# Neighbourhood attention block: squares, bias tables, last product order and residual loads rearranged

## The chip, the cores and the metric

The kernel runs on one core of a Trainium2 chip. The metric is the device time of one execution in microseconds; the time of a kernel is the median of its runs. Inputs and outputs are float32.

## What is computed

One layer of an encoder on 512 tokens (8 rows of 64 columns) of width 2048, with 16 heads of width 128. Cut to what matters:

```python
h = rms_norm(x, norm_pre)
q, k, v, z = split(h @ w_in, 4)            # 2048 -> 4 x 2048
s = q . k * 128**-0.5 + rpb[dr, dc]        # a window of 8 rows x 16 columns per token
o = softmax(s) @ v
y = (o * silu(z)) @ w_out                  # 2048 -> 2048
x = x + rms_norm(y, norm_post)
```

## The kernel before

The two large matrix products make up nearly all the work. Each float32 operand is split into a high part `hi` (a cast on ScalarE, line 241 for weights) and a rest `lo` (a subtraction on VectorE, line 242), and a product is three matmuls of 512 columns per output block: hi·hi, lo of the activations times hi, hi times lo of the weights.

The work is a list of 512 weight tiles of 128x512 (256 KB each), called products here and numbered m. It is cut into ten steps. Step 0 and step 8 are plain (`PLAIN`): 32 products of twelve matmuls each, 16 for each half of the output columns; step 0 computes the first pair of heads, step 8 half of the output product. Steps 1 to 7 (a pair of heads each) and step 9, the last one (`LAST`, products 456 to 511), save an eighth of the matmuls by a seven-product scheme: seven passes of eight products with six matmuls, called A11, S1, A12, N2, A22, N4 and N3 after their left operand (numbers 0 to 6, P1 to P7 in the change's title). They add into three pairs of accumulators X, Y and Z (`chain`, line 258); `combine` (331) reads these at the end of a pass. In the last step the table `LATE` (51) gives the passes another order, A11, S1, N2, A22, N4, N3, A12; its last pass, A12, runs block by block (line 299), and both its operands lie in the tiles `a{k}_2` and `a{k}_3`, whose former contents were used up by then.

Weights come in two ways. A pass that takes a tile of the input as it is (`is_raw`, 205) loads it into one of four buffers `raw` (`load_raw`, 216), about six products ahead, each buffer after the tile four loads earlier has been used. Sums of tiles are kept in eight resident tiles `T[k]`, shown as `t`: passes S1, N2 and A22 add a raw tile to T (line 234) and take the sum; A22 then reloads T (247); N4 uses a raw tile and adds it to T behind its own split (249), and N3 takes that sum. `prep` (227) does all this two products ahead of the matmuls; `hi` and `lo` have three buffers, so a cast waits until the product three before has run.

All loads of weights, activations and residuals are issued by SP in order; an SP instruction that waits holds up those behind it. GpSimd's queue issues the bias rows and the gated outputs. A scheduler orders the instructions of each engine from the program order and its own estimate, so rows stand somewhat off the program's order; engines run their rows in order. Calls through `sync`, `dve` and `act` (`InOrder`, 56) keep their program order.

Beside the products, `at(m, f)` hangs the other work on product m:

- RMSNorm statistics: `square_x` (174) loads x in eight blocks `sq` of 512 KB, and ScalarE squares and sums them. `rstd` (185) makes the factor `rc` from the sums: two small VectorE operations and a power on GpSimd. `take_first` (283) copies step 0's accumulators to SBUF times `rc`: the first half (n = 0) at product 28 and after, the second at 31.
- Bias: `load_bias` (441) loads overlapping rows of a head's table by GpSimd's queue (184 KB); `bias` (447) reverses them, adds a mask and writes the table `bm`, three VectorE operations per head; `add_bias` (472) reads it.
- The end: `finish` (653) squares a block of y, multiplies it by the post-norm gain, and collects the sums; `final` (669) scales it, adds the residual `xres` (16 tiles of 256 KB, names are row block and column block) and stores it. `load_res` (677) issues the residual loads: those of row blocks 2 and 3 with each product of pass S1, of 1 with every second product of N2, of 0 in N3.

Of the kernel before, what the change touches and what calls it, by code (L numbers as in the profile page):

```python
# [15 lines left out]
P = 128  # L16
# [33 lines left out]
B11, B12, B21, B22 = range(4)  # L50
LATE = (0, 1, 3, 4, 5, 6, 2)
NRAW = 4
# [14 lines left out]
@with_exitstack  # L67
def na_block(ctx: ExitStack, tc: tile.TileContext, xT, x, gpre, gpost, w, rpb, mask, out):
    nc = tc.nc
# [29 lines left out]
    nc.gpsimd.memset(mhalf, -0.5)  # L99
    mask_sb = cp.tile([P, 3, 32], F32, name="mask_sb")  # L100
    edge = {}
# [22 lines left out]
    def load_t(step, q, k):  # L124
        nc.sync.dma_start(T[k], w[step, q, k])

# [83 lines left out]
    seq = [m for m in range(N) if is_raw(m)]  # L210
    for i, m in enumerate(seq):
        e = max(m - 6 if m < N - KH else 0, seq[i - NRAW] if i >= NRAW else 0)
        if m > 2:
            at_prep.setdefault(e, []).append(m)

    def load_raw(m):
        raws[m] = wp.tile([P, L], F32, tag="raw", name=f"raw{m}", bufs=NRAW)
        step, p, k = where(m)
        if step in PLAIN:
            src = w[step, (B11, B12, B21, B22)[p + 2 * (k // KH)], k % KH]  # L220
        else:
            src = w[step, (None, B12, B21, B22, B21, B22)[p], k]
        nc.sync.dma_start(raws[m], src)
# [3 lines left out]
    def prep(m):  # L227
        step, p, k = where(m)
        plain = step in PLAIN
        if step == 0 and p == 0:  # L230
            take_x(k)
        src = raws.pop(m) if is_raw(m) else T[k]
        if not plain and p in (1, 3, 4):
            nc.vector.tensor_tensor(T[k], T[k], src, ALU.add)  # L234
# [6 lines left out]
        nc.scalar.copy(hi, src)  # L241
        nc.vector.tensor_tensor(lo, src, hi.bitcast(F32), ALU.subtract)  # L242
# [40 lines left out]
    def take_first(n, j):  # L283
        c = C.setdefault(0, {})
        name = ("11", "12", "21", "22")[n + j // 2 * 2]
        if j % 2 == 0:
            c[name] = pair(f"c{name}_0")
        nc.scalar.activation(c[name][:, j % 2, :], U[n][j], AF.Copy, scale=rc[:, j : j + 1])

# [41 lines left out]
    def combine(step, p):  # L331
# [14 lines left out]
        elif p == 3:  # L346
            c["22"] = pair(f"e_{step}")
            for s in range(2):
                nc.vector.tensor_tensor(c["22"][:, s, :], u[s], c["12"][:, s, :], ALU.subtract)
            nc.vector.tensor_tensor(c["21"], c["22"], c["21"], ALU.subtract)  # L350
        elif p == 4:
            for s in range(2):
                nc.vector.tensor_tensor(c["22"][:, s, :], u[s], c["22"][:, s, :], ALU.add)
        elif p == 5:
            for s in range(2):
                nc.vector.tensor_tensor(c["12"][:, s, :], u[s], c["12"][:, s, :], ALU.subtract)  # L356
            for s in range(2):
                if step == LAST:
                    finish(3, s, c["12"][:, s, :])
                else:  # L360
                    scale_c(c["12"], s, 0)
        elif step == LAST:
            c["11"] = pair(f"c11_{step}")
            for s in range(2):
                dve.tensor_tensor(c["21"][:, s, :], u[s], c["21"][:, s, :], ALU.subtract)
                dve.tensor_tensor(c["22"][:, s, :], c["22"][:, s, :], u[s], ALU.subtract)
                finish(2, 2 + s, c["21"][:, s, :])
                finish(3, 2 + s, c["22"][:, s, :])
# [72 lines left out]
    def load_bias(h):  # L441
        raw = sp.tile([P, L], F32, tag="braw", name=f"braw{h}")
        src = bass.AP(rpb.tensor, rpb.offset + h * 15 * TBL, [[1, 16], [TBL, 8], [1, 7 * TBL + 32]])
        nc.gpsimd.dma_start(raw[:, 0 : 7 * TBL + 32], src)  # L444
        bm_of[h] = (raw, sp.tile([P, 3, 256], F32, tag="bm", name=f"bm{h}"))

    def bias(h, i):
        raw, bm = bm_of[h]
        rev = bass.AP(raw.tensor, raw.offset + 7 * TBL + 31, [raw.ap[0], [-1, 32], [-TBL, 8]])
        nc.vector.tensor_tensor(  # L450
            bm[:, i, :].rearrange("p (a b) -> p a b", b=8),
            rev,
            mask_sb[:, i, :].unsqueeze(2).to_broadcast([P, 32, 8]),
            ALU.add,
        )

# [15 lines left out]
    def add_bias(h, a):  # L472
# [3 lines left out]
        for i in ((0, 1), (3, 2))[a]:  # L476
# [5 lines left out]
                in0=s_of[h, a][:, base + lo : base + hi],  # L482
                in1=bm_of[h][1][:, (0, 1, 1, 2)[i], lo:hi],
                op0=ALU.add,
# [113 lines left out]
    for h in range(HEADS):  # L598
# [3 lines left out]
        at(when(h, 0) - (4 if late else 11), load_bias, h)  # L602
        for i in range(3):
            at(when(h, i) if late else when(h, 0) - 7 + i, bias, h, i)
    for pr in range(NSTEP):
# [47 lines left out]
    def finish(n, t, src, dst=None):  # L653
# [6 lines left out]
        nc.scalar.activation(rest, src, AF.Square, accum_out=part[:, t, i : i + 1])  # L660
        (dve if n > 1 else nc.vector).tensor_tensor(y, src, gb[n], ALU.mult)
        if i == 2:
            nc.vector.reduce_sum(ms3[:, col], part[:, t, 0:3], axis=mybir.AxisListType.X)
            nc.vector.tensor_scalar(ms3[:, col], ms3[:, col], 1.0 / D, EPS, ALU.mult, ALU.add)
        if i == 3:
            dve.tensor_scalar(msy[:, col], part[:, t, 3:4], 1.0 / D, ms3[:, col], ALU.mult, ALU.add)
            nc.gpsimd.tensor_tensor(rcy[:, col], msy[:, col], mhalf[:, 0:1], ALU.pow)

    def final(t):
        col = slice(t, t + 1)  # L670
        for q in range(4):
            r = xres[t, q]
            dve.scalar_tensor_tensor(r, yg[q, t], rcy[:, col], r, ALU.mult, ALU.add)
# [21 lines left out]
    for s in range(2):  # L695
        at(base(LAST) + 6 * KH + 1 + s, final, 2 + s)


    for k in range(3):
        load_x(k)  # L700
        load_raw(k)
    for m in range(-AHEAD, N):
        if m + AHEAD < N - KH:
            prep(m + AHEAD)
        if N - 2 * KH <= m + AHEAD < N - KH:
            prep(m + AHEAD + KH)
        if 0 <= m and m + 3 < KT:
            load_x(m + 3)
        if m < 0:
# [5 lines left out]

def _mask():
    m = np.full((P, 3, GRID_W // 2), NEG, np.float32)
    for typ, i in ((0, 0), (1, 1), (2, 3)):
        for c in range(16):
            col = 16 * i + c  # L720
            lo = min(max(col - KW // 2, 0), GRID_W - KW)
            for kc in range(32):
                key = 16 * i - 8 + kc
                if lo <= key < lo + KW and 0 <= key < GRID_W:
                    m[c * ROWS : (c + 1) * ROWS, typ, kc] = 0.0
    return m

# [38 lines left out]
```

## Time and profile before

| what | us |
|---|---|
| median of 3 runs | 899.44 (899.15 to 900.58) |
| the profiled execution | 903.68 |
| its span, first to last instruction | 901.9 |
| around the span | 1.8 |
| TensorE busy | 880.9 |
| VectorE busy | 755.3 |
| ScalarE busy | 561.2 |
| mean granted TensorE clock | 0.994 of full |

The profile's engines are PE (TensorE matmul), PEld (its weight loads), DVE (VectorE), ACT (ScalarE), POOL (GpSimd) and SP, which only issues DMAs. A timeline row gives start, length, engine, line, operation with out<-in, count, and in brackets the idle time before it and what ended that. A row of windows gives a stretch, its length, the busy time of PE, PEld, DVE, ACT and POOL (in parentheses how many instructions), the granted clock, the mean busy share of the 16 DMA engines, and GB/s. Pages print line 64 for instructions issued through the in-order wrappers.

### The profile page before, as it was taken

The page shows a single profiled execution, that of the slowest core. Times are in us where ns is not written, and L with a number is a line of the kernel's source. Part 1 is how long each engine was busy: PE and PEld are TensorE (multiplying, and loading weights), DVE is VectorE, ACT ScalarE, POOL GpSimd, SP SyncE. Part 2 cuts the span into 40 slices and gives each one's busy share as a digit, 9 for nine tenths or more (in the row PEclk, how much of TensorE's full clock was granted, in tenths as well). Part 3 has the DMA queues.
Part 4 walks back from the last instruction along what each step waited for, and adds up shares of the span by engine and source line. Part 5 has one row for each costly group of instructions (what it writes and reads, how often), then busy time and mean ns, then how long its engine had stood idle before and what let it go on. Part 6 is the DMA issues. An engine that isn't in the chain of part 4 may idle for free. (4 is left out here: it accounts for less than half of the span.)

```text
span 901.9 us, 13169 instructions
## 1 busy us (share of the span) xinstructions
PE 880.9 (98%) x4184; PEld 731.3 (81%) x4184; DVE 755.3 (84%) x1415; ACT 561.2 (62%) x1089; POOL 29.7 (3%) x59
## 2 busy tenths in 40 slices
PE   9999999999999999999999999999999999999994
PEld 7878888888888888888888888888888788887773
DVE  5467879997989798989888987998799855887987
ACT  7566766575758575856585667566766755554461
POOL 1000000000000000000000000000010100000001
PEclk9999999999999999999999999999999999999998
DMA  8895357745773776377647764765587534549765
GB/s 256 237 258 131 105 138 210 217 130 162 219 214 111 190 227 192 95 218 210 176 112 219 210 176 110 239 200 149 137 278 205 157 93 119 158 122 254 245 179 186
DMA packets 85878, 163.32 MB, mean 181 GB/s; under 512 B 10017, under 2 KB 10017, under 8 KB 85809
## 3 DMA queue, kind: packets, MB, share of 16 engines
q1 hardware_dynamic: 82080, 151.56, 57.7%
q0 software_dynamic: 3296, 10.41, 4.2%
q8 instruction: 32, 0.52, 0.2%
q10 hardware_dynamic: 432, 0.53, 0.2%
q14 instruction: 38, 0.30, 0.1%
HBM read 154.59 MB, written 7.86 MB: 180 GB/s over the span
## 5 line engine op out<-in xcount | busy, mean ns | idle before, releaser
L241 ACT CAST hi<-t 128x512 fp32r<-128x512 f32 x320 | 196.8, 618 | 137.3 <-DVE lo L242 31.1
L242 DVE TENSOR_TENSOR lo<-t,hi 128x512 fp32r<-128x512 f32 x320 | 218.1, 687 | 25.8 <-ACT hi L241 24.9
L242 DVE TENSOR_TENSOR lo<-raw,hi 128x512 fp32r<-128x512 f32 x184 | 125.8, 689 | 62.8 <-ACT hi L241 50.3
L241 ACT CAST hi<-raw 128x512 fp32r<-128x512 f32 x184 | 113.6, 620 | 98.9 <-PE u L279 18.7
L234 DVE TENSOR_TENSOR t<-t,raw 128x512 f32<-128x512 f32 x192 | 128.5, 688 | 13.0 <-DMA raw<-in_w 12.5
L279 PE MATMUL u<-hi,a 128*128 128x512 f32 x512 | 133.1, 397 | 3.4 <-ACT hi L241 2.1
L279 PEld LDWEIGHTS u<-hi,a 128*128 128x128 f32 x512 | 96.2, 191 | 24.3 <-ACT hi L241 2.6
L279 PE MATMUL u<-lo,a 128*128 128x512 f32 x256 | 70.8, 390 | 0.0
L279 PEld LDWEIGHTS u<-lo,a 128*128 128x128 f32 x256 | 48.2, 188 | 10.1
L249 DVE TENSOR_TENSOR t<-t,raw 128x512 f32<-128x512 f32 x64 | 42.8, 688 | 1.2 <-DMA raw<-in_w 1.1
L149 DVE TENSOR_TENSOR a<-x,a 128x256 fp32r<-128x256 f32 (+1 forms) x24 | 11.6, 512 | 19.5 <-ACT a L148 19.5
L450 DVE TENSOR_TENSOR bm<-braw,mask_sb 128x256 f32<-128x256 f32 x48 | 27.4, 601 | 0.0
L322 PE MATMUL u1Y<-hi,a 128*128 128x512 f32 x96 | 26.8, 396 | 0.0
L322 PE MATMUL u6Y<-hi,a 128*128 128x512 f32 x96 | 26.8, 396 | 0.0
L322 PE MATMUL u5Y<-hi,a 128*128 128x512 f32 x96 | 26.8, 396 | 0.0
L322 PE MATMUL u7Y<-hi,a 128*128 128x512 f32 x96 | 26.8, 396 | 0.0
L322 PE MATMUL u3Y<-hi,a 128*128 128x512 f32 x96 | 26.8, 396 | 0.0
L322 PE MATMUL u4Y<-hi,a 128*128 128x512 f32 x96 | 26.8, 396 | 0.0
L322 PE MATMUL u2Y<-hi,a 128*128 128x512 f32 x96 | 26.8, 396 | 0.0
L322 PE MATMUL u9Y<-hi,a 128*128 128x512 f32 x96 | 26.6, 392 | 0.0
L444 POOL DMA_DIRECT2D braw<-in_rpb x16 | 8.5, 534 | 437.9 <-DVE bm L450 253.5
L322 PEld LDWEIGHTS u9Y<-hi,a 128*128 128x128 f32 x96 | 17.9, 188 | 4.3 <-ACT s L341 0.4
(444 smaller groups left out, 1953.2 us busy)
## 6 DMA issues: line engine op xcount, KB each, us to landing
raw<-in_w SPq DMA_DIRECT2D x384, 256.0 KB, 3.0
t<-in_w SPq DMA_DIRECT2D x128, 256.0 KB, 3.0
x<-in_xT SPq DMA_DIRECT2D x16, 256.0 KB, 4.4
xres<-in_x SPq DMA_DIRECT2D x16, 256.0 KB, 6.2
graw<-zm POOLq DMA_DIRECT2D x14, 256.0 KB, 3.7
out<-xres SPq DMA_DIRECT2D x14, 256.0 KB, 3.2
sq<-in_x SPq DMA_DIRECT2D x6, 512.0 KB, 9.4
braw<-in_rpb POOLq DMA_DIRECT2D x16, 184.0 KB, 3.6
```

What stands on the lines that cost most here:

```text
L149: (vector or nc.vector).tensor_tensor(lo, src, hi.bitcast(F32), ALU.subtract)
L234: nc.vector.tensor_tensor(T[k], T[k], src, ALU.add)
L241: nc.scalar.copy(hi, src)
L242: nc.vector.tensor_tensor(lo, src, hi.bitcast(F32), ALU.subtract)
L249: nc.vector.tensor_tensor(T[k], T[k], src, ALU.add)
L279: nc.tensor.matmul(U[n][j], l, r, start=k == 0 and i == 0, stop=k == KT - 1 and i == 2)
L322: nc.tensor.matmul(U[c][s], l, r, start=p in (0, 1, 4) and k == 0 and n == 0, stop=k == KH - 1 and n == 2, skip_group_check=True,)
L444: nc.gpsimd.dma_start(raw[:, 0 : 7 * TBL + 32], src)
L450: nc.vector.tensor_tensor(bm[:, i, :].rearrange("p (a b) -> p a b", b=8), rev, mask_sb[:, i, :].unsqueeze(2).to_broadcast([P, 32, 8]), ALU ...
```

## The change

Five things change.

1. In step 0 the squares begin four products later (10 instead of 6) and stand five products after their load instead of six; one more input tile is loaded ahead, and bias tables and squares no longer stand among the first inputs. The first half's accumulators are copied plain at product 17 and after, and multiplied by `rc` at 31. The loads of T for step 1 keep program order among the `sync` calls.
2. The bias tables are laid out in memory before the launch (reversed, with the mask in them); a head's `bm`, 384 KB, is one load on SP. The three VectorE operations per head, the mask and the rows' buffer are gone.
3. The last step's passes run A11, S1, N2, A22, N3, N4, A12. N3, now ahead of N4, loads the tiles that N4 loads as well, adds them to T itself, and N4 no longer does.
4. The splits for A12 (`late_prep`), which stood one with each product of the pass before A12, now stand one with every second product of the two passes before it. The raw loads follow that order.
5. Residual tiles of row blocks 2 and 3 load every three and a half products from S1 on, those of 1 and 0 later; those of 0 go into T. The finishing of row blocks 2 and 3 moves from the end of N3 into N4, and their final additions with it. Several VectorE calls may be reordered now (`nc.vector` instead of `dve`).

The diff, cut to its core:

```diff
-LATE = (0, 1, 3, 4, 5, 6, 2)
+LATE = (0, 1, 3, 4, 6, 5, 2)
...
-        return step in PLAIN or p not in (0, 6)
+        return step in PLAIN or p not in (0, 6) or step == LAST and p == 6
+
+    def late_prep(m):
+
+        i, odd = divmod(m - (N - 3 * KH + 1), 2)
+        return [N - KH + i] if 0 <= i < KH and not odd else []
...
-        if not plain and p in (1, 3, 4):
+        if not plain and (p in (1, 3, 4) or step == LAST and p == 6):
             nc.vector.tensor_tensor(T[k], T[k], src, ALU.add)
...
-        elif p == 5:
+        elif p == 5 and step < LAST:
             nc.vector.tensor_tensor(T[k], T[k], src, ALU.add)
...
-        nc.scalar.activation(c[name][:, j % 2, :], U[n][j], AF.Copy, scale=rc[:, j : j + 1])
+        if n == 0:
+
+            nc.scalar.copy(c[name][:, j % 2, :], U[n][j])
+        else:
+            nc.scalar.activation(c[name][:, j % 2, :], U[n][j], AF.Copy, scale=rc[:, j : j + 1])
...
     def load_bias(h):
-        raw = sp.tile([P, L], F32, tag="braw", name=f"braw{h}")
...
+        bm_of[h] = sp.tile([P, 3, 256], F32, tag="bm", name=f"bm{h}")
+        nc.sync.dma_start(bm_of[h], rpb[h])
...
-        at(6 + 2 * i, begin, i)
-        at(12 + 2 * i, lambda i=i: pending.pop(i)())
-    at(8, lambda: nc.gpsimd.dma_start(mask_sb, mask))
-    at(28, rstd)
+        at(10 + 2 * i, begin, i)
+        at(15 + 2 * i, lambda i=i: pending.pop(i)())
+    at(30, rstd)
     for j in range(4):
-        at(28 + j, take_first, 0, j)
+        at(KT + 1 + j, take_first, 0, j)
+        at(FIRST - 1, lambda j=j: scale_c(C[0][("11", "21")[j // 2]], j % 2, j // 2 * 2))
...
-            if q % 2 == 0:
-                xres["c", q] = ag.tile([P, 2, L], F32, tag=f"a{q // 2}_1", name=f"xres{t}{q}")
-            xres[t, q] = xres["c", q - q % 2][:, q % 2, :]
+            xres[t, q] = T[q]
...
-    for k in range(KH):
-        t, q = divmod(k, 4)
-        at(base(LAST) + KH + k, load_res, 2 + t, q)
-        at(base(LAST) + (5 * KH + 2 * q + 1 if t == 0 else 2 * KH + 2 * q), load_res, t, q)
+    for i, (t, q) in enumerate((t, q) for t in (2, 3, 1) for q in range(4)):
+        at(base(LAST) + (KH + 7 * i // 2 if i < KH else 4 * KH + 4 + 2 * q), load_res, t, q)
+    for q in range(4):
+        at(base(LAST) + 5 * KH + q, load_res, 0, q)
     for s in range(2):
-        at(base(LAST) + 6 * KH + 1 + s, final, 2 + s)
+        for n, key in ((2, "21"), (3, "22")):
+            at(base(LAST) + 5 * KH + 1 + 2 * s, lambda n=n, key=key, s=s: finish(n, 2 + s, C[LAST][key][:, s, :]))
+        for q in range(4):
+            at(base(LAST) + 5 * KH + 5 + 2 * s + q // 2, final, 2 + s, (q,))
```

ScalarE's rows at the seam from step 0 to step 1, before (`sq` are the squares, `c11` to `c22` the copies of step 0's accumulators, `hi31` the last cast of step 0, a number behind the last underscore is a buffer):

```order
L241 CAST hi31_886<-raw31_799 128x512
L241 CAST hi32_910<-t0_143 128x512
L64 CAST a7_3_142<-x6_280 128x2x256
L241 CAST hi33_930<-t1_144 128x512
L288 ACTIVATE c12_0_949<-u0_1_0_586,rc_108 128x512
L288 ACTIVATE c12_0_949<-u0_1_1_587,rc_108 128x512
L389 CAST vh0_0_984<-c12_0_949 128x512
L288 ACTIVATE c22_0_952<-u0_1_2_588,rc_108 128x512
L288 ACTIVATE c22_0_952<-u0_1_3_589,rc_108 128x512
L64 CAST a7_1_140<-x15_499 128x2x256
L241 CAST hi34_958<-t2_145 128x512
```

The same place now:

```order
L247 CAST hi31_884<-raw31_801 128x512
L64 ACTIVATE sq7_792,part_108<-sq7_792 128x1024
L64 CAST a6_1_135<-x14_445 128x2x256
L387 ACTIVATE c11_0_618<-c11_0_618,rc_107 128x512
L247 CAST hi32_908<-t0_142 128x512
L387 ACTIVATE c11_0_618<-c11_0_618,rc_107 128x512
L387 ACTIVATE c21_0_668<-c21_0_668,rc_107 128x512 x2
L64 CAST a7_3_141<-x6_256 128x2x256
L247 CAST hi33_929<-t1_143 128x512
L298 ACTIVATE c12_0_951<-u0_1_0_579,rc_107 128x512
```

The last square and the four scalings now stand between hi31 and hi33; the copies of the second half and hi34 follow as before.

VectorE's rows where the last step goes from A22 to its next pass, before (`e_9<-u9Z` is the combination behind A22; lo488 to lo495 belong to the next pass, `a0_2` to `a7_2` are the splits for A12):

```order
L242 TENSOR_TENSOR lo488_8932<-raw488_8881,hi488_8931 128x512
L242 TENSOR_TENSOR lo489_8945<-raw489_8895,hi489_8944 128x512
L353 TENSOR_TENSOR e_9_8841<-u9Z0_8853,e_9_8841 128x512
L353 TENSOR_TENSOR e_9_8841<-u9Z1_8854,e_9_8841 128x512
L242 TENSOR_TENSOR lo490_8960<-raw490_8909,hi490_8959 128x512
```

Now:

```order
L240 TENSOR_TENSOR t1_143<-t1_143,raw489_8821 128x512
L248 TENSOR_TENSOR a0_2_112<-raw504_8835,a0_3_113 128x512
L248 TENSOR_TENSOR lo486_8831<-t6_148,hi486_8830 128x512
L240 TENSOR_TENSOR t2_144<-t2_144,raw490_8849 128x512
L248 TENSOR_TENSOR lo487_8845<-t7_149,hi487_8844 128x512
L240 TENSOR_TENSOR t3_145<-t3_145,raw491_8864 128x512
L248 TENSOR_TENSOR lo488_8861<-t0_142,hi488_8860 128x512
L248 TENSOR_TENSOR a1_2_116<-raw505_8877,a1_3_117 128x512
L248 TENSOR_TENSOR lo489_8874<-t1_143,hi489_8873 128x512
L363 TENSOR_TENSOR e_9_8765<-u9Z0_8777,e_9_8765 128x512
L363 TENSOR_TENSOR e_9_8765<-u9Z1_8778,e_9_8765 128x512
```

Additions of raw tiles to T and two splits for A12 now stand ahead of the combination.

SP's rows in the same stretch, before (t0 to t7 are the loads of T, raw488 to raw503 weights of the two passes, raw504 to raw511 those of A12):

```order
L125 DMA t7_150<-in_w 128x512
L223 DMA raw492_8936<-in_w 128x512
L223 DMA raw493_8949<-in_w 128x512
L223 DMA raw494_8964<-in_w 128x512
L223 DMA raw495_8977<-in_w 128x512
L223 DMA raw504_8990<-in_w 128x512
L223 DMA raw505_9003<-in_w 128x512
```

Now:

```order
L124 DMA t7_149<-in_w 128x512
L229 DMA raw493_8896<-in_w 128x512
L64 DMA xres33_8904<-in_x 128x1x512
L229 DMA raw506_8911<-in_w 128x512
L229 DMA raw494_8915<-in_w 128x512
L229 DMA raw495_8928<-in_w 128x512
L229 DMA raw507_8941<-in_w 128x512
L229 DMA raw496_8945<-in_w 128x512
L229 DMA raw497_8958<-in_w 128x512
L64 DMA xres10_8966<-in_x 128x1x512
```

Weights of the running pass and of A12 now take turns, with residual tiles among them.

More of the change, by code (lines that the diff above doesn't have):

```diff
@@ L67, in na_block @@
 @with_exitstack
-def na_block(ctx: ExitStack, tc: tile.TileContext, xT, x, gpre, gpost, w, rpb, mask, out):
+def na_block(ctx: ExitStack, tc: tile.TileContext, xT, x, gpre, gpost, w, rpb, out):
     nc = tc.nc
@@ L124, in load_t @@
     def load_t(step, q, k):
-        nc.sync.dma_start(T[k], w[step, q, k])
+        (sync if step == 1 and q == B11 else nc.sync).dma_start(T[k], w[step, q, k])
     X = {}
@@ L206, in is_raw @@
         step, p, _ = where(m)
-        return step in PLAIN or p not in (0, 6)
+        return step in PLAIN or p not in (0, 6) or step == LAST and p == 6
+    def late_prep(m):
+        i, odd = divmod(m - (N - 3 * KH + 1), 2)
+        return [N - KH + i] if 0 <= i < KH and not odd else []
     raws, at_prep = {}, {}
-    seq = [m for m in range(N) if is_raw(m)]
+    preps = [j for m in range(N - KH) for j in [m] + late_prep(m)]
+    place = {m: i for i, m in enumerate(preps)}
+    seq = [m for m in preps if is_raw(m)]
     for i, m in enumerate(seq):
-        e = max(m - 6 if m < N - KH else 0, seq[i - NRAW] if i >= NRAW else 0)
-        if m > 2:
-            at_prep.setdefault(e, []).append(m)
+        e = max(place[m] - 6, place[seq[i - NRAW]] if i >= NRAW else 0)
+        if i > 2:
+            at_prep.setdefault(preps[e], []).append(m)
     def load_raw(m):
@@ L221, in load_raw @@
         else:
-            src = w[step, (None, B12, B21, B22, B21, B22)[p], k]
+            src = w[step, (None, B12, B21, B22, B21, B22, B22)[p], k]
         nc.sync.dma_start(raws[m], src)
@@ L602, in na_block @@
         at(when(h, 0) - (4 if late else 11), load_bias, h)
-        for i in range(3):
-            at(when(h, i) if late else when(h, 0) - 7 + i, bias, h, i)
     for pr in range(NSTEP):
@@ L665, in finish, with final @@
         if i == 3:
-            dve.tensor_scalar(msy[:, col], part[:, t, 3:4], 1.0 / D, ms3[:, col], ALU.mult, ALU.add)
+            nc.vector.tensor_scalar(msy[:, col], part[:, t, 3:4], 1.0 / D, ms3[:, col], ALU.mult, ALU.add)
             nc.gpsimd.tensor_tensor(rcy[:, col], msy[:, col], mhalf[:, 0:1], ALU.pow)
-    def final(t):
+    def final(t, qs=range(4)):
         col = slice(t, t + 1)
-        for q in range(4):
+        for q in qs:
             r = xres[t, q]
-            dve.scalar_tensor_tensor(r, yg[q, t], rcy[:, col], r, ALU.mult, ALU.add)
+            nc.vector.scalar_tensor_tensor(r, yg[q, t], rcy[:, col], r, ALU.mult, ALU.add)
             eng = nc.scalar if t == 1 and q % 2 else nc.sync
@@ L704, in na_block @@
             prep(m + AHEAD)
[L705 to L708, printed above, removed]
+            for j in late_prep(m + AHEAD):
+                prep(j)
+        if 0 <= m and m + 4 < KT:
+            load_x(m + 4)
         if m < 0:
@@ L762 @@
     with tile.TileContext(nc) as tc:
-        na_block(tc, *(aps[k] for k in ("xT", "x", "gpre", "gpost", "w", "rpb", "mask")), out)
+        na_block(tc, *(aps[k] for k in ("xT", "x", "gpre", "gpost", "w", "rpb")), out)
     r = run_bass_kernel_spmd(nc, [{f"in_{k}": v for k, v in feeds.items()}], core_ids=[0])
```

45 lines of the change are left out of this document (17 added, 28 removed).

## The prediction

> **What bounds the kernel now.** I read the busy times of the page first, then the windows of three stages, to learn which engine sets the time and where that engine stands idle.
>
> ```profile
> span 901.9 us, 13169 instructions
> PE 880.9 (98%) x4184; PEld 731.3 (81%) x4184; DVE 755.3 (84%) x1415; ACT 561.2 (62%) x1089; POOL 29.7 (3%) x59
> ```
>
> ```profile
> 0.00:60.00 60.00, 56.33 (x239) 46.77 (x240) 29.60 (x56) 37.33 (x70) 2.70 (x12) 0.97 0.87 251
> 60.00:800.00 740.00, 738.75 (x3580) 616.44 (x3579) 641.12 (x1214) 479.46 (x934) 24.36 (x43) 1.00 0.60 172
> 800.00:902.00 102.00, 85.82 (x369) 68.14 (x367) 84.63 (x146) 44.42 (x86) 2.63 (x4) 0.96 0.70 202
> ```
>
> TensorE (first column behind the length) is idle for 21 us of 901.9: 3.7 us before 60 us, 1.25 us in the 740 us between, 16.2 us after 800. So nothing in the heads' middle steps can be worth more than 1.25 us, and only both ends matter. There I read TensorE's timeline. First the one stop of the opening step, where eight matmuls go from 42.73 to 44.55, so a product of twelve takes 2.72 us:
>
> ```profile
> 42.73 1.98 PE L279 MATMUL u<-hi,a 128*128 128x512 f32 x8
> 44.55 1.07 PE L279 MATMUL u<-lo,a 128*128 128x512 f32 x4
> 47.75 3.69 PE L279 MATMUL u<-hi,a 128*128 128x512 f32 x8 [2.13 <-ACT hi L241]
> ...
> 54.93 1.98 PE L279 MATMUL u<-hi,a 128*128 128x512 f32 x8
> ```
>
> ```profile
> 44.00:48.00 4.00, 1.87 (x9) 1.25 (x8) 0.96 (x2) 2.06 (x4) 0.00 (x0) 0.97 1.01 247
> 48.00:52.00 4.00, 4.00 (x12) 3.14 (x13) 2.32 (x4) 3.87 (x8) 0.00 (x0) 0.60 0.71 215
> ```
>
> Product 13 begins at 42.73 and product 16 at 54.93: 12.20 us for three products of 2.72, a loss of 4.04 us. Only 2.13 us of it is the wait; the rest is the granted clock of 0.60 after it (eight matmuls in 3.69 us where they took 1.98). The wait is ScalarE's, and ScalarE was waiting for inputs, with the DMA share at 1.0:
>
> ```profile
> 46.47 0.72 ACT L159 ACTIVATE x<-x,gcol 128x512 f32<-128x512 f32 x1 [1.94 <-DMA x<-in_xT]
> 47.09 0.60 ACT L241 CAST hi<-raw 128x512 fp32r<-128x512 f32 x1
> ```
>
> The second place is the last step, seven passes of eight products. The starts of its passes S1 (818.06), A22 (844.49), N4, N3 and A12, with one wait in between:
>
> ```profile
> 818.06 1.07 PE L322 MATMUL u9Y<-hi,a 128*128 128x512 f32 x4
> ...
> 836.19 0.74 PE L322 MATMUL u9Y<-lo,a 128*128 128x512 f32 x2 [1.16 <-DVE lo L242]
> ...
> 844.49 1.07 PE L322 MATMUL u9Z<-hi,a 128*128 128x512 f32 x4
> 855.37 1.07 PE L322 MATMUL u9Y<-hi,a 128*128 128x512 f32 x4
> 866.25 1.07 PE L322 MATMUL u9Z<-hi,a 128*128 128x512 f32 x4
> 878.29 0.61 PE L322 MATMUL u9X<-a,a 128*128 128x512 f32 x2
> ```
>
> A free pass is 10.88 us (844.49 to 855.37), a product 1.36. S1 and N2 take 26.43 us, 4.67 too many; N3 takes 12.04, 1.16 too many. In S1 and N2 VectorE waits for weights while the DMA engines are full (share 1.02); afterwards share, rate and landing fall:
>
> ```profile
> 814.00:838.00 24.00, 21.68 (x89) 15.86 (x87) 16.32 (x27) 10.98 (x19) 0.00 (x0) 1.00 1.02 271
> 838.00:862.00 24.00, 23.55 (x104) 19.50 (x105) 23.09 (x38) 10.67 (x18) 0.00 (x0) 1.00 0.73 228
> ```
>
> ```profile
> 832.00 0.69 DVE L234 TENSOR_TENSOR t<-t,raw 128x512 f32<-128x512 f32 x1 [1.60 <-DMA raw<-in_w]
> ```
>
> The third is the tail. VectorE's own queue, not TensorE's end, sets it: the first row block's product is done before 884.0, but its scaling by the gain (c, 889.30) stands behind eight residual additions.
>
> ```profile
> 855.08:897.62 42.54, 33.51 (x146) 26.90 (x145) 37.99 (x71) 17.81 (x38) 2.63 (x4) 0.96 0.61 183
> ```
>
> ```profile
> 877.81 0.69 DVE L64 TENSOR_TENSOR s<-u9Z,s 128x512 f32<-128x512 f32 x1 [0.82 <-PE u9Z L322]
> ...
> 889.30 0.68 DVE L64 TENSOR_TENSOR c<-u9X,gpost 128x512 f32<-128x512 f32 x1
> ...
> 894.87 1.42 DVE L64 SCALAR_TENSOR_TENSOR xres<-y,rcy,xres 128x512 f32<-128x512 f32 x2 [0.66 <-POOL rcy L667]
> ...
> 896.87 0.75 DVE L64 SCALAR_TENSOR_TENSOR xres<-s,rcy,xres 128x512 f32<-128x512 f32 x1
> ```
>
> From the end of the A22 pass to 897.62 VectorE is busy 37.99 of 42.54 us. From there to the span's end only stores remain (4.3 us), before and after.
>
> **The change, part by part.** All terms go against the profiled execution, 903.68 us (span 901.9 and 1.8 around it). That run lies 4.2 us above the median of 899.44; I carry the difference in us over to the median. A difference under 0.2% (1.8 us) counts as none.
>
> *Opening step, first half.* Ahead of the load of raw17 stood four blocks of squares (2 MB), now one (0.5 MB) and the first bias table (384 KB); x14, issued behind raw15 before, now goes ahead of raw12, and x15, behind raw16 before, ahead of raw14. So I let the wait and its clock go: **-4.0** (bounds -4.0 and 0: the same transfer at the same share of 1.0, but with less ahead of it; I take the first, since a wait of 2.13 us is what four fewer transfers have to cover).
>
> The Trainium skill ("TensorE: Matmul & The Clock Gate", Part 1: The HAM clock gate) has the clock fall only after an idle window of about 3.4 us; by that rule the wait would cost no clock, the term would be -2.1 and the sum -4.3. The row with 0.60 says otherwise, and the row decides.
>
> *Opening step, second half.* The squares come later, and the four copies of the first half lose their factor, which four more scalings apply at the seam to step 1. The seam before:
>
> ```profile
> 83.19 0.15 DVE L186 TENSOR_REDUCE ms<-part 128x4 f32<-128x8 f32 x1
> ```
>
> ```profile
> 85.31 1.26 ACT L288 ACTIVATE c<-u,rc 128x512 f32<-128x512 f32 x2 [1.66 <-POOL rc L188]
> ...
> 96.61 1.37 ACT L288 ACTIVATE c<-u,rc 128x512 f32<-128x512 f32 x2 [0.91 <-PE u L279]
> ...
> 100.19 1.67 ACT L241 CAST hi<-t 128x512 fp32r<-128x512 f32 x3
> ```
>
> ```profile
> 98.45 1.07 PE L322 MATMUL u1X<-hi,a 128*128 128x512 f32 x4
> ```
>
> From the row sums to ScalarE's first scaled copy go 2.1 us (83.19 to 85.31), through GpSimd. Now the last square stands behind hi31, which needs the buffer of product 28, free at 98.45 - 3 x 2.72 = 90.29. hi31 (0.55) and the square (1.1) end at 91.95, the factor is there at 94.1. Then ScalarE's queue holds four scalings and three casts ahead of the copies of the second half:
>
> ```profile
> L379 ACT ACTIVATE s<-s,rc x28: 707/716/724, 175.4 to 711.6; 128x512 f32<-128x512 f32 x28
> ```
>
> With 0.63 from start to start of a scaling and 0.55 of a cast that is 4.2 us, to 98.3; the four copies with their two casts take what they took, 96.61 to 100.19, so hi34 starts at 101.9 and ends at 102.45. TensorE needs it at 98.45 + 2 x 1.36 = 101.17: a new wait of **+1.3** (bounds 0, if a cast or two slip ahead, and 4.0, if the squares' loads are late). The last block's load waits for lo27, some 10 us before its square:
>
> ```profile
> DMA to landing us min/median/max: 6.2/9.4/9.5
> ```
>
> That just covers. Loads of t3 to t7 go behind it, and have until 102.
>
> *Bias.* 48 vector additions go:
>
> ```profile
> L450 DVE TENSOR_TENSOR bm<-braw,mask_sb x48: 578/601/617, 13.9 to 725.9; 128x256 f32<-128x256 f32 x48
> ```
>
> That is 28.8 us of VectorE, nearly all of it beside a TensorE that idles 1.25 us in those 740. The loads double to 384 KB and move from GpSimd's queue to SP's, where the weights behind them would wait if the table were still read; its last reader stands at least four products ahead of them, so the wait is over (in the last pair only one, but there a product lasts 2.72 us and the weight behind has several to spare). **0** (bounds -1.25 and +1.4, 14 tables by 0.1 of raw landing).
>
> *Last step, S1 and N2.* Twelve residual loads stood among these passes' weights; now four or five do. Demand is 16 weights and 4.6 residual tiles of 0.262 MB in 21.76 us, 248 GB/s, against the 271 that the full engines moved. **-4.3** of the 4.67 (the other bound -2, since 248 is close).
>
> *Last step, N3 in place of N4.* N3 now follows A22 in the same accumulators, and the combination behind A22 has to read them first. In VectorE's queue that stands behind lo489 and the split of raw505, so it can start 0.7 us after the pass where it started 0.3 us before; TensorE's four hoisted matmuls of A12 cover 0.9 us. The stall of some 0.6 us costs nothing by itself, since VectorE sets the end: its queue from there counts 56 wide operations where it counted 58 (two splits for A12 went ahead): -1.3 at 0.63 each; the 0.82 us wait at 877.81 goes, since the rows' finishing is spread; the later start costs +1.0. Together **-1.1**. The residual additions are the same sixteen, the two waits for GpSimd stay, and the stores that move forward stand on SP behind the last weight, so they hold nothing up.
>
> *Last step, the ring of four.* N3 now loads its weights a second time, and the splits for A12 begin a pass earlier: 24 weights pass through four buffers in two passes, where 16 did. Landing before:
>
> ```profile
> DMA to landing us min/median/max: 2.6/3.3/7.3
> ```
>
> ```profile
> DMA to landing us min/median/max: 2.6/3.0/3.4
> ```
>
> (820 to 875, and 845 to 875). A buffer's turn is landing plus a cast (0.62), a split (0.69) and an issue (0.33): at 3.3 us 4.94, a weight every 1.235 us. Nineteen must be loaded into reused buffers, the first some 4.5 us ahead of the passes: 23.5 us against 21.76 + 4.5 = 26.3. At 4.3 us of landing it is 28.2, or **+1.9**, which I take, between 0 (3.3) and +16.2 (7.3), nearer the first: from the load of t0 on there are 38 loads (10 MB) in 34 us, 293 GB/s, where share 0.73 moved 228 and share 1.02 moved 271 with every second load a residual.
>
> The Trainium skill ("DMA: Bandwidth & Descriptors", Specifications) gives one core about 358 GB/s of HBM; by it the ring would not slow and the sum would be -8.1. No run here moves that much, and the 271 row stands against it.
>
> Sum: -4.0 + 1.3 + 0 - 4.3 - 1.1 + 1.9 = -6.2, so 899.44 - 6.2 = **893.2**; the profiled execution 897.5.
>
> **The rivals.** *Slower: the ring starves.* For: TensorE waits in both passes once landing grows, and 271 GB/s at full share is below the demand of 293. Against: after 845 landing kept under 3.4. Without the ring the sum is -8.1; slower than 0.2% needs +9.9, a landing of 6.0 us. At 6.5 it is +12.4, so 903.7. *It cancels.* The same with landing between 5.2 and 6.0; at 5.5 it is +7.6, so 898.9. *The opening step gives all back.* The seam costs one product more (4.0), or ScalarE, whose queue now takes x13 and x14 ahead of hi10, waits earlier for the same data: -3.5, so 895.9. For: the 10 us of cover and a landing of 9.4. Against: fewer bytes before it. *All gains, no price.* Neither seam nor ring costs: -4.0 - 4.67 - 1.1 = -9.8, so 889.6.
>
> **How the numbers follow.** Forecast 0.42, opening step gives back 0.17, all gains 0.15: faster, 0.74. Cancels: the same, 0.12. Starved: slower, 0.14. The range from 888.5 to 900.0 reaches from just below the best case over the cancelling one and leaves out the starved ring.
>
> **What would show it.** Right: products 13 to 16 of the opening step at 2.72 us with the clock at 1.0; S1 and N2 of 10.9 us each; in the opening step's last products ScalarE's casts behind the scalings, and a TensorE wait of 1 to 2 us at the third product of step 1; DMA landing of weights near 4 us in N3 and N4; the last residual addition about 42 us after the end of A22. Wrong: landing above 5 us and TensorE waiting for lo or hi all through N3 and N4; a wait in products 9 to 14; a tail that ends on TensorE's last product with VectorE already free.

## The result and the profile after

The changed kernel takes 896.61 us (median of 17 runs, 894.44 to 897.76), the kernel before 900.59 (17 runs, 899.15 to 905.83). The ratio is 0.9946 [0.9934, 0.9958], or 4.9 us less (3.8 to 5.9), where the forecast was 6.2. The means (901.4 and 896.5) differ by as much, the medians by only 4.0: five of the 17 runs of before take over 902.5 us, none of after does, and a median doesn't see them. The profiled execution of after took 896.13 us, its span 894.4: 7.5 less than the span of before that the prediction worked from. First the page of after, span and busy times:

```profile
span 894.4 us, 13143 instructions
PE 877.7 (98%) x4184; PEld 729.3 (82%) x4184; DVE 733.8 (82%) x1367; ACT 560.7 (63%) x1093; POOL 21.0 (2%) x42
```

VectorE lost 21.5 us of work, and TensorE is as full as it was. The windows of the three stages:

```profile
0.00:60.00 60.00, 58.74 (x262) 49.29 (x263) 30.68 (x58) 40.07 (x76) 0.91 (x9) 1.00 0.77 230
60.00:800.00 740.00, 737.92 (x3576) 615.58 (x3576) 622.10 (x1171) 478.23 (x935) 16.96 (x29) 1.00 0.59 179
800.00:894.50 94.50, 81.03 (x349) 64.44 (x347) 81.02 (x138) 42.41 (x83) 3.17 (x4) 0.97 0.77 236
```

TensorE's idle time fell from 3.7 to 1.3 us in the first window and from 16.2 to 13.5 in the last; between them it grew from 1.25 to 2.1, although the bias work is gone from VectorE. TensorE's timeline of the opening step, products 0, 1, 13, 14 and 16, and the seam to step 1:

```profile
5.97 2.11 PE L285 MATMUL u<-hi,a 128*128 128x512 f32 x8 [0.20 <-ACT hi L247]
...
8.82 1.98 PE L285 MATMUL u<-hi,a 128*128 128x512 f32 x8
...
41.46 1.98 PE L285 MATMUL u<-hi,a 128*128 128x512 f32 x8
...
44.18 1.98 PE L285 MATMUL u<-hi,a 128*128 128x512 f32 x8
...
49.62 1.98 PE L285 MATMUL u<-hi,a 128*128 128x512 f32 x8
...
93.14 1.07 PE L332 MATMUL u1X<-hi,a 128*128 128x512 f32 x4
...
96.31 1.19 PE L332 MATMUL u1X<-hi,a 128*128 128x512 f32 x4 [0.29 <-ACT hi L247]
```

From product 13 to 16 it is 8.16 us, three times 2.72: the stop of 4.04 us is gone. At the third product of step 1 stands the forecast wait for ScalarE's cast, but the product starts 0.45 us late (96.31 against 93.14 + 2.72), not 1.3. The last step, starts of S1, A22 and N3, and the stops:

```profile
813.46 1.07 PE L332 MATMUL u9Y<-hi,a 128*128 128x512 f32 x4
...
835.51 1.07 PE L332 MATMUL u9Z<-hi,a 128*128 128x512 f32 x4
...
849.07 1.33 PE L332 MATMUL u9Z<-hi,a 128*128 128x512 f32 x4 [1.43 <-DVE e L363]
...
865.00 0.73 PE L332 MATMUL u9Y<-lo,a 128*128 128x512 f32 x2 [0.98 <-DVE lo L248]
...
872.26 1.19 PE L332 MATMUL u9Y<-hi,a 128*128 128x512 f32 x4 [0.48 <-ACT hi L247]
```

S1 and N2 take 22.05 us (26.43 before; 21.76 would be free of waits). Behind A22, which ends at 846.39, N3 waits 1.43 us for the combination, and N4 stops twice. The stretch from there to the last residual addition at 890.10, the landing of weights from 811 to 872, and in the stretch VectorE's waits and ScalarE's waits for the weights of A12:

```profile
846.39:890.10 43.71, 34.64 (x145) 26.37 (x143) 37.83 (x70) 17.86 (x38) 3.17 (x4) 0.99 0.80 244
```

```profile
DMA to landing us min/median/max: 2.7/3.8/5.9
```

```profile
DVE a L248 <- ACT a L247: 4.0, 4, 2.0
DVE xres L668 <- POOL rcy L662: 0.7, 1, 0.7
DVE t L668 <- POOL rcy L662: 0.7, 1, 0.7
```

```profile
ACT a L247 <- DMA raw<-in_w: 11.0, 6, 2.4
```

(Such a row gives who waited for what: us in total, times, longest.) VectorE is busy 37.83 us, and 37.70 in before's stretch cut the same way (855.37 to 897.62), but the stretch is 1.5 us longer than before's 42.25: 4.0 us go to four splits for A12 that wait for their casts, and these for their loads.

Every run below is cut the same way, us in the profiled execution. With A22 itself (10.88) and the stores (4.3) a row adds up to the span.

| run | product 1 starts | opening, to step 1 | steps 1 to 8 | A11, S1, N2 | end of A22 to last addition |
|---|---|---|---|---|---|
| before | 9.96 | 98.5 | 708.7 | 37.3 | 42.3 |
| before again | 10.16 | 95.1 | 707.0 | 38.9 | 41.9 |
| after | 8.82 | 93.1 | 709.4 | 32.9 | 43.7 |
| opening step alone | 10.13 | 94.7 | 708.1 | 38.7 | 42.7 |
| bias alone | 8.79 | 93.1 | 707.6 | 38.0 | 42.8 |
| last step alone | 10.62 | 95.9 | 707.4 | 32.9 | 44.9 |
| bias and residual loads | 8.59 | 93.0 | 707.8 | 33.0 | 41.1 |
| after, five buffers | 9.04 | 93.5 | 706.4 | 33.0 | 42.4 |
| mask late | 9.73 | 94.2 | 707.5 | 37.4 | 43.8 |
| rows late | 8.60 | 97.0 | 707.7 | 38.4 | 43.1 |
| bias, residuals, five buffers | 8.79 | 93.5 | 706.4 | 33.0 | 43.0 |
| opening, bias, residuals | 8.65 | 93.0 | 710.1 | 32.9 | 41.1 |

### The profile page after: what moved, and what is told of

Its sections match the earlier page's. It is cut to its first block, busy times and chain, and to the rows that moved or that the text cites. A ratio compares the mean times of both kernels' runs of the same rounds, so it can differ in the third digit from the quotient of the medians.

```text
span 894.4 us, 13143 instructions
## 1 busy us (share of the span) xinstructions
PE 877.7 (98%) x4184; PEld 729.3 (82%) x4184; DVE 733.8 (82%) x1367; ACT 560.7 (63%) x1093; POOL 21.0 (2%) x42
## 5 line engine op out<-in xcount | busy, mean ns | idle before, releaser
L247 ACT CAST hi<-t 128x512 fp32r<-128x512 f32 x320 | 196.6, 618 | 132.2 <-DVE lo L248 21.5
L285 PE MATMUL u<-hi,a 128*128 128x512 f32 x512 | 130.9, 392 | 1.4 <-DVE e L380 1.2
L285 PEld LDWEIGHTS u<-hi,a 128*128 128x128 f32 x512 | 94.9, 188 | 21.5 <-DVE e L380 1.8
L255 DVE TENSOR_TENSOR t<-t,raw 128x512 f32<-128x512 f32 x56 | 37.3, 686 | 7.3 <-DMA raw<-in_w 7.3
L545 POOL DMA_DIRECT2D graw<-zm x14 | 7.8, 554 | 561.7 <-DVE zm L539 561.7
L495 ACT ACTIVATE edge<-edge,nm 128x192 f32<-128x192 f32 x32 | 14.5, 455 | 8.7 <-DVE nm L488 8.7
L332 PEld LDWEIGHTS u4Y<-hi,a 128*128 128x128 f32 x96 | 17.4, 188 | 3.2
```

Of the source, the lines that this page charges most:

```text
L285: nc.tensor.matmul(U[n][j], l, r, start=k == 0 and i == 0, stop=k == KT - 1 and i == 2)
L332: nc.tensor.matmul(U[c][s], l, r, start=p in (0, 1, 4) and k == 0 and n == 0, stop=k == KH - 1 and n == 2, skip_group_check=True,)
L495: nc.scalar.activation(p, p, AF.Exp, bias=nm[:, i : i + 1], accum_out=sm[:, i : i + 1])
L545: nc.gpsimd.dma_start(graw[h], z_of[h])
```

## The experiments

### Before again

The kernel before, unchanged, with a second profile.

> The kernel before, unchanged, profiled a second time. Theory: its profiled execution (903.7 us) was longer than its median because the two DMA-bound stops, product 14 of the opening step (4.0 us) and passes S1 and N2 (4.7 us), were longer in it than usual; then this profile runs 899 to 902 us and the two stops together cost 5 to 7 us instead of 8.7. Rival: both stops are always as long and the extra time of that execution lies elsewhere; then the stops again cost 8.5 to 9 us whatever the time.

900.12 us (12 runs), ratio 1.0003 [0.9985, 1.0021]; the profiled execution 899.9. Its opening step, products 13 and 14:

```profile
42.94 1.98 PE L279 MATMUL u<-hi,a 128*128 128x512 f32 x8
...
46.03 2.11 PE L279 MATMUL u<-hi,a 128*128 128x512 f32 x8 [0.21 <-ACT hi L241]
```

Here the stop costs 0.4 us for one product and no clock. S1 and N2 lose 6.3 us instead of 4.67, for here a wait in N2 is long enough to cost the clock (0.50 for the 3 us after it):

```profile
832.20 1.22 PE L322 MATMUL u9Y<-lo,a 128*128 128x512 f32 x2 [2.20 <-DVE lo L242]
```

So the first profile's stop of 4.04 us is not in every execution of this kernel. How many have it isn't known: no other long execution was profiled.

### The three parts alone

Opening step alone: the edits of point 1 in the kernel before.

```diff
-        at(6 + 2 * i, begin, i)
-        at(12 + 2 * i, lambda i=i: pending.pop(i)())
+        at(10 + 2 * i, begin, i)
+        at(15 + 2 * i, lambda i=i: pending.pop(i)())
...
+        at(KT + 1 + j, take_first, 0, j)
```

> Only the opening step is changed (squares later, first half copied plain and scaled at the seam, one more input tile ahead). Theory: this alone takes away the stop at product 14, leaves a wait of about 0.5 us at the third product of step 1, and moves product 1 little; S1 and N2 keep their stops. 2.5 to 4.5 us faster than before. Rival: the stop depends on the bias rows and the mask as well and comes back in part; then under 1.5 us.

899.75 us, ratio 0.9987 [0.9971, 1.0003]: 1.2 us less by the ratio, 0.6 by the medians (900.3 before), with no change inside the interval. The gain that I expected isn't there: the stop is gone (product 14 starts at 45.72, 2.72 us after product 13), but in most executions it was small to begin with. The time is in the rival's band; its mechanism isn't, for nothing of the stop came back.

What the opening step may do is end the long executions. Of 86 executions of before, 19 lie more than 1.9 us above the median of those run with them, up to 5.2 us; of the 40 of the four kernels with this opening step none lies more than 1.8 us above its median. That the long ones are those with the stop fits the one that was profiled, but isn't shown.

Bias alone: the tables from memory (point 2).

```diff
-        nc.gpsimd.dma_start(raw[:, 0 : 7 * TBL + 32], src)
+        nc.sync.dma_start(bm_of[h], rpb[h])
...
-            at(when(h, i) if late else when(h, 0) - 7 + i, bias, h, i)
...
-    at(8, lambda: nc.gpsimd.dma_start(mask_sb, mask))
```

> Only the bias tables are laid out in memory and loaded by SP. Theory: 28 us less VectorE work is worth nothing, because TensorE is idle 1.25 us in those 740 us: within 1.5 us of before. It takes the two small transfers away that stood among the first loads, so product 1 starts about 1 us earlier (8.8 instead of 10.0 us), and the stop at product 14 takes that back. Rival: VectorE's load holds back TensorE without a visible wait; then 3 us or more faster, with the gain between 60 and 800 us.

897.93 us, ratio 0.9971 [0.9955, 0.9987]: 2.6 us faster, where at most 1.5 was expected. It is not VectorE's relief, since steps 1 to 8 are no shorter (707.6 us) than in the second profile of before (707.0). The opening step is shorter, by 2.0 us: TensorE's products 0 and 1 before, and then with the bias alone:

```profile
6.19 2.38 PE L279 MATMUL u<-hi,a 128*128 128x512 f32 x8
...
9.96 2.11 PE L279 MATMUL u<-hi,a 128*128 128x512 f32 x8 [0.49 <-ACT a L148]
```

```profile
5.95 2.09 PE L278 MATMUL u<-hi,a 128*128 128x512 f32 x8
...
8.79 1.98 PE L278 MATMUL u<-hi,a 128*128 128x512 f32 x8
```

Product 1 starts 1.2 us earlier, and the stop at product 14 is gone as well.

Last step alone: points 3 to 5 in the kernel before.

```diff
-LATE = (0, 1, 3, 4, 5, 6, 2)
+LATE = (0, 1, 3, 4, 6, 5, 2)
...
+            if i < KH else 4 * KH + 4 + 2 * q
```

> Only the last step is changed (order A11 S1 N2 A22 N3 N4 A12, splits for A12 spread, residual loads spread, finishing moved). Theory: S1 and N2 run free (10.9 to 11.2 us each, 3 to 4.4 us less), and from the end of A22 to the last residual addition it takes about 43.7 us instead of 42.25, so 1 to 3 us faster than before. Rival: the new order and the spread finishing free the tail as well; then 4 us or more faster.

897.9 us, ratio 0.9968 [0.995, 0.9985], 2.9 us faster, as expected. The stretch up to A22 is 6.0 us shorter than in the second profile of before, and the one behind A22 3.0 longer: the second effect takes back half of the first.

### Which load held up the start

Before, GpSimd's queue issued the first head's bias rows and the mask at the start. In the one kernel the mask goes to SP, in the other the first head's rows do:

```diff
-    at(8, lambda: nc.gpsimd.dma_start(mask_sb, mask))
+    at(8, lambda: sync.dma_start(mask_sb, mask))
```

> The kernel before; only the load of the mask (48 KB, rows of 384 bytes) goes to SP behind the second block of squares instead of standing at the start. Theory: the overlapping bias rows slow the first weights, not the small mask: product 1 starts at 9.8 to 10.3 us as before. Rival: the mask does; then product 1 starts at 8.8 us.

```diff
-        nc.gpsimd.dma_start(raw[:, 0 : 7 * TBL + 32], src)
+        (nc.gpsimd if h else sync).dma_start(raw[:, 0 : 7 * TBL + 32], src)
```

> The kernel before; only the first head's bias rows (184 KB) go to SP at the end of the opening step instead of GpSimd's queue at the start. Theory: product 1 starts at 8.8 to 9.2 us, as with the bias tables in memory, and the DMA rate between 5 and 7 us stays above 300 GB/s. Rival: no change, 9.8 to 10.3 us.

One run each, 899.88 and 903.08 us. The landing of the weights issued between 5 and 9.5 us, in before, with the mask late (one load each) and with the rows late (two):

```profile
DMA to landing us min/median/max: 5.1/5.1/5.1
```

```profile
DMA to landing us min/median/max: 4.9/4.9/4.9
```

```profile
DMA to landing us min/median/max: 2.7/3.0/3.3
```

Product 1 starts at 9.73 without the mask and at 8.60 without the rows: it is the rows. The engines move 335 GB/s from 5 to 7 us without them, 220 in before. Whether it is the rows' bytes, their overlapping form or GpSimd's queue was not separated. That kernel loses its gain at 60 us, where VectorE meets the first bias addition, and TensorE behind it; VectorE's row, then TensorE's:

```profile
59.84 0.58 DVE L450 TENSOR_TENSOR bm<-braw,mask_sb 128x256 f32<-128x256 f32 x1 [8.62 <-DMA braw<-in_rpb]
```

```profile
57.80 1.97 PE L279 MATMUL u<-hi,a 128*128 128x512 f32 x8
61.67 1.46 PE L279 MATMUL u<-lo,a 128*128 128x512 f32 x4 [1.90 <-DVE lo L242]
62.93 3.35 PE L279 MATMUL u<-hi,a 128*128 128x512 f32 x8
```

So its 903.08 says where a late table hits, not what an early one costs.

### The old order with the other gains

Bias from memory and residual loads spread as in the change, with the old order of passes, splits, finishing and opening step:

```diff
-        at(base(LAST) + KH + k, load_res, 2 + t, q)
-        at(base(LAST) + (5 * KH + 2 * q + 1 if t == 0 else 2 * KH + 2 * q), load_res, t, q)
+        at(base(LAST) + KH + 7 * k // 2, load_res, 2 + t, q)
+        at(base(LAST) + (5 * KH + 2 * q + 1 if t == 0 else 4 * KH + 4 + 2 * q), load_res, t, q)
```

> The kernel before with the bias tables in memory and the residual loads spread as in the change; the last step keeps its old pass order, splits and finishing, the opening step is as before. Theory: S1 and N2 run free here too (10.9 to 11.3 us each), because the spread loads alone cure them, and from the end of A22 to the last residual addition it takes 41.9 to 43 us as before, since the 1.5 to 2.5 us that the change lost there come from the new order with 24 weights in the ring. So 2 to 3 us faster than the changed kernel (6 to 8 us faster than before). Rival: the residual tiles that moved into N4 and N3 cost that stretch the same 1.5 to 2.5 us whatever the order; then as fast as the changed kernel, within 1 us.

891.97 us (6 runs, beside 900.1 for before), ratio 0.9914 [0.9896, 0.9933]: faster than the whole change, as expected. The stretch behind A22, its window and VectorE's waits:

```profile
844.70:885.80 41.10, 32.83 (x145) 26.83 (x143) 37.55 (x70) 17.95 (x38) 2.63 (x4) 0.96 0.73 213
```

```profile
DVE t L248 <- DMA raw<-in_w: 1.6, 2, 0.9
DVE xres L64 <- POOL rcy L651: 1.3, 2, 0.7
DVE s L64 <- ACT ysq L644: 0.5, 2, 0.3
```

VectorE works as long as in after (37.55 and 37.83) and idles 2.3 us less. The new order saves it nothing and adds waits; S1 and N2 owe their gain to the residual loads alone.

The same with the opening step of the change, so that only the new order and what goes with it (points 3 and 4, the moved finishing) is missing:

```diff
-    at(28, rstd)
+    at(30, rstd)
     for j in range(4):
+        at(KT + 1 + j, take_first, 0, j)
```

> The whole change without the new pass order, its splits and its finishing: opening step, bias and spread residual loads. Theory (the opening step of the change is worth its own stop, which typical runs show as 0.5 us, and costs 0.3 to 0.5 at the seam; the order is what the change loses by): 891 to 892.5, the same as without the opening step (891.97) within 1 us. Rival (the opening step is worth the 4 us that the profiled execution before showed): 888 to 889.5. Rival 2 (the seam costs 1.3 as forecast, the stop nothing): 893 to 894.

893.18 us (beside 900.33), ratio 0.9917 [0.9903, 0.9931]. Its window behind A22:

```profile
846.91:888.01 41.10, 32.82 (x145) 26.84 (x143) 37.47 (x70) 17.96 (x38) 2.63 (x4) 0.96 0.73 214
```

Again 41.10, 2.6 below the 43.71 of after, and by the ratios (0.9917 and 0.9946, their intervals apart) this kernel is 2.6 us faster than the full change. The stretch of a single profile is a loose measure: the six profiles that have the last step of before unchanged give 41.9 to 43.8 us. Beside the bias change the opening step brings nothing that these runs can tell: 0.9917 against 0.9914. The time itself falls into the band of the second rival, but that one's mechanism does not show, since the seam again waits 0.30 us. The profiled span exceeds that of the kernel without it by 2.0 us, all of it in steps 1 to 8 (710.1 against 707.8).

### A fifth raw buffer

```diff
-NRAW = 4
+NRAW = 5
```

In the changed kernel:

> The changed kernel with five buffers for raw weights instead of four. Theory (the ring): the last stretch is long because a weight's buffer comes free too late; with five buffers the waits of ScalarE for raw weights in N3 and N4 (2.4, 2.1 and 2.4 us) shrink, and the stretch from the end of A22 to the last residual addition falls from 43.7 to 41 to 42.5 us: 1 to 2.5 us faster than the changed kernel. Rival (VectorE's own queue): the order of its operations sets the stretch; then it stays within 0.5 us of 43.7.

891.81 us (5 runs, beside 900.1), ratio 0.9906 [0.9888, 0.9924]: more than expected. Behind A22 the window, the landing from 811 to 872 and VectorE's waits:

```profile
843.68:886.06 42.38, 34.19 (x145) 26.37 (x143) 36.84 (x69) 16.41 (x36) 3.77 (x4) 0.97 0.81 238
```

```profile
DMA to landing us min/median/max: 2.8/4.0/6.2
```

```profile
DVE lo L248 <- ACT hi L247: 2.3, 4, 1.1
DVE a L248 <- ACT a L247: 1.9, 2, 1.3
```

```profile
ACT a L247 <- DMA raw<-in_w: 9.7, 5, 2.8
```

The stretch is 1.3 us shorter, but not by the expected cause: the loads land no sooner (4.0 against 3.8), and ScalarE waits as long for raw weights (9.7 us for A12's and 3.5 for the others, where it was 11.0 and 1.6). VectorE's work in the stretch is 1.0 us less, with one operation fewer in it, and its idle time 0.3. That the ring made this stretch long isn't shown, then, and 1.3 us is less than single profiles of one last step differ.

Steps 1 to 8 are 3.0 us shorter too, and there the ring does show. The waits for raw weights in these steps, in after and with five buffers:

```profile
ACT hi L247 <- DMA raw<-in_w: 16.8, 17, 1.5
DVE t L255 <- DMA raw<-in_w: 7.3, 7, 1.4
DVE t L240 <- DMA raw<-in_w: 4.8, 11, 0.8
```

```profile
DVE t L240 <- DMA raw<-in_w: 2.3, 8, 0.4
```

With five buffers steps 2 to 7 take 86.8 us each; with four, after needs up to 87.7 (step 5).

And in the old order, with bias and residual loads:

> The kernel before with the bias in memory, the spread residual loads and five raw buffers, in the old pass order with the old finishing. In the changed kernel a fifth buffer was worth 4 us, of which its two traces put 1.3 behind the A22 pass and 3.0 in the steps 1 to 8. Theory (what the fifth buffer mends behind A22 is the new order's doubled weights, 24 through four buffers; in the steps 1 to 8 it is worth something in any order): here only the second part is left, so 889 to 891, 1 to 3 us below the same kernel with four buffers, and the stretch from the end of A22 to the last residual addition stays within 0.7 us of its 41.1. Rival (the fifth buffer shortens the last step in any order): 887.5 or less, that stretch near 39.5. Rival 2 (a fifth buffer's gain is chance of the schedule): within 0.8 us of 891.97.

893.02 us (beside 900.33), ratio 0.9921 [0.9903, 0.994], no better than with four (0.9914). Steps 1 to 8 are 1.4 us shorter, as the theory had it (the waits for raw weights there fall from 22.3 to 2.7 us), but the stretch behind A22 grows, against the theory:

```profile
843.76:886.72 42.96, 33.42 (x145) 26.69 (x143) 37.22 (x69) 17.75 (x38) 2.62 (x4) 0.94 0.70 199
```

So a gain from five buffers shows only with the new order; why not here stays open. The best two kernels, the change with five buffers (0.9906) and the old order with bias and residual loads (0.9914), cannot be told apart.

## Why the prediction was right, and where it was not

The direction was right, the time lies within the range, and the gain of S1 and N2 came as forecast. Most other terms were mis-sized, and they offset one another: that the sum came so near is in part luck.

*Opening step, first half (-4.0): wrong size.* What failed is the sentence "I carry the difference in us over to the median". The profiled execution lay 4.2 us above its median, and I counted its stop of 4.04 us as a property of the kernel. The second profile shows the stop at 0.4, and the opening step makes 3.3 of the 3.8 us between the two (98.5 and 95.1 in the table; the later stages nearly cancel). The part alone is worth 1.2 us at 0.9987 [0.9971, 1.0003].

*Seam (+1.3): right mechanism, too dear.* It measures 0.45 us, in the same place and behind the same queue. The factor came earlier than I had it: 5.0 us before step 1 (the first scaling starts at 88.15 by ScalarE's timeline, step 1 at 93.14), where I had 4.35 (94.1 and 98.45).

*Bias (0): wrong, it gains 2.6 us (1.2 to 4.0).* That the 28.8 us of VectorE (its busy time fell by 21.5) are worth nothing fits the runs. What failed was to weigh the loads only where they go, on SP, and not where they come from: the rows' load of 184 KB ran beside the first weights, whose landing goes from 5.1 to 3.0 us without it. On SP the tables are not free either. The step "so the wait is over" failed: in after, between 100 and 790 us, the table loads on SP wait ten times for the table's reader (line 476):

```profile
SPq L451 <- DVE mx L476: 25.3, 10, 4.1
```

And the waits for raw weights in steps 1 to 8 grow from 6.2 us (before again) to 15.6 with the bias alone and 28.9 in after. The largest come once in each of steps 1 to 7, in pass N4, 5 to 13 us behind the load of a table. Little of this reaches TensorE.

*S1 and N2 (-4.3): right.* 26.43 to 22.05, 4.38 less; against the second profile of before it is 6.0, part of which is the clock that its wait of 2.20 us cost. Spreading the residual loads does this in either order.

*N3 in place of N4 (-1.1) and the ring (+1.9): the sum of +0.8 measured +1.5, and the comparison behind it was too kind.* With the same residual loads the old order takes 41.1 us behind A22, so the new order costs 2.6 us there. The -1.3 for two operations fewer failed: VectorE's busy time behind A22 is 37.83 us, where it was 37.70. The stall after A22 is 1.43 us, not 0.6: the split of raw505, ahead of the combination, waits 0.96 us for its cast, and that had waited 2.43 us for its load. The ring turned at a landing of 3.8 us, below my 4.3, and by my formula would have cost nothing there; I had spread a median landing over 19 loads, while single loads take up to 5.9 us and a cast that waits for one holds VectorE's queue behind it. Since a fifth buffer left these waits as long, it is open whether the four buffers made the loads late. Nor was the 271 GB/s a ceiling, on which the forecast of slower landing leaned: from 5 to 7 us the kernel with the bias alone moves 383.

*Steps 1 to 8 (nothing forecast): 0.7 us longer than in the first profile of before, 2.4 longer than in the second,* the seam's 0.45 among it. The step "nothing in the heads' middle steps can be worth more than 1.25 us" failed: with five buffers steps 1 to 8 take 706.4 us in both kernels, 2.3 less than in the first profile of before (0.6 less than in the second), and TensorE's busy time there falls from 707.5 to 705.9, so the idle time of that profile was no bound. One wait can be named, at the first product of step 8:

```profile
705.82 0.72 PE L285 MATMUL u<-hi,a 128*128 128x512 f32 x2 [1.16 <-DVE e L380]
```

It is 0.74 and 0.45 in the two profiles of before, 1.1 to 1.2 in the four kernels that have the bias from memory and four buffers, 0.19 and 0.48 in the two with five. Another stands in step 5 of after and of the kernel without the new order (0.36 and 0.51 us, at 487.77 and 487.91), behind a VectorE operation that had waited for a raw weight (0.48 and 1.35 us). How the rest divides is open: kernels with the opening step of the change and four buffers take 708.1 to 710.1 us there, the others with four 707.0 to 708.7, too near to each other for one profile of each to settle.

Of the rivals, "the opening step gives all back" (895.9) came nearest to the 896.61, by another road: neither of its two prices was paid, but there was little to gain. The starving ring came true in kind, with stops of TensorE and VectorE behind late weights, but the price was 2.6 us behind A22 and not 12.4. By the table the change against the second profile of before is -2.0 (opening) + 2.4 (steps 1 to 8) - 6.0 (S1 and N2) + 1.8 (behind A22) = -3.8, its span's 898.1 to 894.4.

## What to carry to other kernels

Before pricing a stop from one profile, compare that run with its median: an excess the size of the stop says that the stop may belong to the run. Compare the spread of the runs too, since a change that removes such a stop may show there and not in the median. When a load goes away, look at what ran beside it where it stood, above all in the first microseconds. Test parts of a change alone: here spread loads and a table in memory, without the new order of passes, are worth 7.7 us; the order costs 2.6 with four buffers, and with five these runs can't tell whether it gains.

## What the runs showed of the hardware

A wait of 1.90 us was enough to halve TensorE's clock (rows late, 61.67); the windows of that kernel from 62 us on:

```profile
62.00:63.00 1.00, 1.00 (x5) 0.77 (x4) 1.00 (x4) 0.00 (x0) 0.00 (x0) 0.71 0.35 51
63.00:66.00 3.00, 3.00 (x9) 2.35 (x8) 3.00 (x8) 1.73 (x4) 0.54 (x1) 0.53 0.50 107
66.00:68.00 2.00, 2.00 (x11) 1.60 (x10) 1.93 (x5) 1.51 (x3) 0.00 (x0) 1.00 0.79 195
```

The clock falls to 0.53 for about 3 us. In after, the wait of 1.43 us at 849.07 left it at 1.00:

```profile
848.90:850.70 1.80, 1.63 (x6) 1.16 (x7) 1.80 (x4) 0.26 (x1) 0.00 (x0) 1.00 1.07 263
850.70:853.40 2.70, 2.70 (x13) 2.25 (x12) 1.99 (x4) 1.59 (x4) 0.00 (x0) 1.00 0.75 251
```

With the 2.13 us of before (0.60 over 4 us) and the 2.20 of before again (0.60 over 4 us), all three waits of about 2 us have cost the clock; the longest that did not is 1.47 us (last step alone, 873.82). The Trainium skill ("TensorE: Matmul & The Clock Gate", Part 1: The HAM clock gate) has it fall after an idle window of about 3.4 us; all three measurements lie below that.
